# The opening of a hybrid diffusion layer: tokens loaded ahead of the scale tiles, tiles prepared ahead of the modulation's copies, shorter pauses of the side work

## The chip, the cores and the metric

One core of a Trainium2 chip runs the whole kernel. The metric is device time in microseconds, the median of three runs. The engines are TensorE (PE, its weight loads PEld), VectorE (DVE), ScalarE (ACT), GpSimd (POOL) and SyncE (SP), which here only issues DMAs. Each engine works through its own instructions in order.

## The reference

One layer over 256 latent tokens and 256 context tokens of width 2048, all in float32. Latent tokens are modulated by a vector `c`, context tokens by `c_ctx`; with one layer only the latent stream is returned. What the change touches is the start:

```python
sh1, sc1, g1, sh2, sc2, g2 = split(silu(c) @ w_ada + b_ada, 6)       # 2048 x 12288 weights
csh1, csc1, ...            = split(silu(c_ctx) @ w_ada + b_ada, 6)
h_l = (rmsnorm(x,   norm_mix) * (1 + sc1)  + sh1)  @ w_in            # 2048 x 9312
h_c = (rmsnorm(ctx, norm_mix) * (1 + csc1) + csh1) @ w_in
# latent attention and gated DeltaNet on the columns, gates, output projection,
x = x + g1 * y
x = x + g2 * conv_glu(rmsnorm(x, norm_ffn) * (1 + sc2) + sh2)        # hidden width 5504
```

## The kernel before

The width of 2048 is cut into 16 tiles of 128 rows, called tile k below. Tokens lie transposed, width on the partitions. Weights and activations are split into a high part (rounded to the matmul's format) and a low part (the rest), and a product is three matmuls: high x high, high x low, low x high.

*Opening.* `cv`, the two conditioning vectors, lands; ScalarE makes `cth` (a tanh), VectorE makes `sc` (the silu). `spread(s, q)` lays a quarter of stream s's vector out along the free axis on TensorE, and it is copied to `scb`: by VectorE for s = 0, by ScalarE for s = 1. `square` squares token quarters (`xl` latent, `xc` context), `square_sum` sums them over the width into `pss`, then come a copy `bc`, sums `msp`, a power step on GpSimd and `bc_ps`, the factors of the norm on all partitions.

*Modulation of tile pairs.* Shifts and scales of the first norm are computed here too, from 32 MB of weights. `mod_mm` multiplies four loads (`raws`, 0.5 MB each) by the vectors into `amp` and copies the row out (`row`, ScalarE); `mod_cols` sums its columns into partitions with sixteen small matmuls per half and writes `shs` or `aas` (ScalarE). This gives the shifts of a pair of tiles, and for the pairs in `SCP` (tiles 0, 1, 4, 5, 8, 9, 12, 13) also the scales (`scale_mm`). The other tiles get their scales from VectorE: `scale_dot(k, s)` is a dot product over a 1 MB tile `wt` for one stream, and `scale_fin(k)` puts bias and norm weight on the two results.

*First projection.* A loop over k. `first_hi(k)` casts the tile's weights `gr` to `gh` (ScalarE). `h_prep(k)` multiplies `xl` and `xc` by scale and norm (VectorE), makes `gl` (VectorE), the high parts of `H` with the shift (ScalarE), and the low parts (VectorE). `first_mm(k, ..., a, b)` is products a to b of the seven output tiles, each for both streams, 14 groups of three matmuls. In iteration k the kernel casts the weights of tile k+1, does two products, the products of one shift or scale group, two more products, that group's `mod_cols`, the last three products, and only then `scale_fin` and `h_prep` of tile k+1, the dots due (`dots`) and the next loads (`loads`).

*Order.* TensorE, the copies and dots of this part, and its loads go through wrappers that keep them in program order on their engine (`pe`, `oact`, `odve`, `osync`); the rest of the kernel is ordered by a planner. `load` asks for a scale tile ("w", 1 MB, four buffers), a shift group ("s", four of five 0.5 MB buffers) or a tile of the first projection's weights ("g", 0.43 MB, three buffers); all wait in SP's queue, in order, for their buffers. SP also has at most a handful of loads under way at once.

*Side work.* `ada_rest` computes the other four modulation vectors: 128 loads `rawa` of 0.5 MB, each one dot product on VectorE against one half of the scale vector, `sch`, which is loaded anew at tiles 0, 16, 48, 80 and 112. It is a generator, run in small steps beside the rest of the kernel: each `yield 1300` is a step, and callers pay for steps with `ada(ns)`. Before and after a change of the half it yields without work. 96 of the 128 dots have to be done when the output projection ends (`while ada.done < 3: ada(1)`), and `ada(WO)` after each of its 16 tiles pays for that.

The lines as the profile names them (a helper that records every operation stands as L68):

Of the kernel before, what the change touches and what calls it, by code (L numbers as in the profile page):

```python
# [25 lines left out]
N1 = 3  # L26
# [13 lines left out]
ADS = 0.3  # L40
OD = 8000
OC = 4000
WO = 2000
IK = 7000
NW = 4
SCP = (0, 2, 4, 6)
# [7 lines left out]
def hybrid_block(ctx: ExitStack, tc: tile.TileContext, io, dbg=None):  # L54
# [46 lines left out]
    dve.tensor_copy(onesr, ones.broadcast_to([P, P]))  # L101
    half = const.tile([P, 1], F32, name="half")
    dve.memset(half, -0.5)
    def vectors(pl, name, names, queue=sync):
        t = pl.tile([P, io[name].shape[1]], F32, name=name)
        queue.dma_start(t, io[name])
        pos, d = 0, {}
        for nm, n in names:
            d[nm] = t[:, pos : pos + n]
            pos += n  # L110
        return d

    off = vectors(const, "vecs", VECS, act)
    nmix, nffn, qan, kvan = off["norm_mix"], off["norm_ffn"], off["q_a_norm"], off["kv_a_norm"]
    bada = off["b_ada"]

# [136 lines left out]
    def ada_rest():  # L253


        def load(i):
            w = wr.tile([P, GR], F32, tag="raw", name="rawa", bufs=NR)
            c, n = divmod(i, 32)
            sync.dma_start(w, io["wada2"][c, (n // 16 + c) % 2, n % 16])
            return w  # L260

        parts = ad.tile([P, 2, 16], F32, name="parts")
        half, ahead = None, load(0)
        for i in range(128):
            c, n = divmod(i, 32)
            h, j = (n // 16 + c) % 2, n % 16
            if h != half:

                for _ in range(2 if i else 0):
                    yield 1300  # L270
                half, sch = h, ad.tile([P, GR], F32, tag="sch", name="sch")
                sync.dma_start(sch, Sc[h])
                for _ in range(4):
                    yield 1300
            w = ahead
            if i < 127:
                ahead = load(i + 1)
            dve.tensor_tensor_reduce(out=w, in0=w, in1=sch, scale=1.0, scalar=0.0, op0=ALU.mult, op1=ALU.add, accum_out=parts[:, h, j : j + 1])  # L278
            if n == 31:
                cs = slice(16 * c, 16 * c + 16)  # L280
                dve.tensor_tensor(out=adaT[:, cs], in0=parts[:, 0], in1=parts[:, 1], op=ALU.add)
                dve.tensor_tensor(out=adaT[:, cs], in0=adaT[:, cs], in1=bada[:, 32 + 16 * c : 48 + 16 * c], op=ALU.add)
                ada.done = c + 1
            yield 1300
# [34 lines left out]
    def spread(s, q):  # L319
        bp = psm.tile([P, 4, P], F32, tag="mm", name="scp")  # L320
        for j in range(4):
            pe.matmul(bp[:, j], sc[:, 4 * q + j, s : s + 1].broadcast_to([P, P]), ident, start=True, stop=True)
        (oact.copy if s else odve.tensor_copy)(scb[:, s, q * 512 : q * 512 + 512], bp.rearrange("p a b -> p (a b)"))
# [21 lines left out]
    def mod_cols(p, scale, amp, row):  # L345

        for j in range(2):
            col_sum(amp[:, T + 2 * j : T + 2 * j + 2], row[:, j * P : (j + 1) * P], sel[:, :2])
        for j in range(2):
            k = slice(2 * p + j, 2 * p + j + 1)  # L350
            out, mul, add = (aas, nmix[:, k], b1[:, k]) if scale else (shs, 1.0, bada[:, k])
            oact.activation(out[:, 2 * p + j], amp[:, T + 2 * j : T + 2 * j + 2], AF.Identity, bias=add, scale=mul)
# [8 lines left out]
    def scale_dot(k, s):  # L361
# [2 lines left out]
            scm[k] = pa2.tile([P, 2], F32, tag="scm", name="scm")  # L364
        junk = ad.tile([P, D], mybir.dt.bfloat16, tag="sch", name="junk")
        odve.tensor_tensor_reduce(out=junk, in0=wts[k], in1=scb[:, s], scale=1.0, scalar=0.0, op0=ALU.mult, op1=ALU.add, accum_out=scm[k][:, s : s + 1])

    def scale_fin(k):
        oact.activation(aas[:, k], scm.pop(k), AF.Identity, bias=b1[:, k : k + 1], scale=nmix[:, k : k + 1])

    def load_first(k):
        gr = pa2.tile([P, G3], F32, tag="gr", name="gr", bufs=3)
# [3 lines left out]
    def first_hi(k):  # L376

        g = [pa2.tile([P, G3], F32R, tag=n, name=n) for n in ("gh", "gl")]
        oact.copy(g[0], grs[k])
        return g  # L380

    def h_prep(k, gh, gl):

        late = k and k % 2 == 0 and k // 2 in SCP
        if late:
            odve.tensor_tensor(out=gl, in0=grs.pop(k), in1=gh, op=ALU.subtract)
        for s, xs in enumerate((xl, xc)):
            odve.scalar_tensor_tensor(out=xs[:, k], in0=xs[:, k], scalar=aas[:, k, s : s + 1], in1=(bc if k else bcp)[:, s], op0=ALU.mult, op1=ALU.mult)
        if not late:
            odve.tensor_tensor(out=gl, in0=grs.pop(k), in1=gh, op=ALU.subtract)  # L390
        for s, xs in enumerate((xl, xc)):
            oact.activation(H[s][:, k, 0], xs[:, k], AF.Identity, bias=shs[:, k, s : s + 1], scale=1.0)
        for s, xs in enumerate((xl, xc)):
            odve.scalar_tensor_tensor(out=H[s][:, k, 1], in0=xs[:, k], scalar=shs[:, k, s : s + 1], in1=H[s][:, k, 0], op0=ALU.add, op1=ALU.subtract)

    def first_mm(k, gh, gl, a, b):
        for j, (o, m) in list(enumerate(FW))[a:b]:
            hi, lo = gh[:, o : o + m], gl[:, o : o + m]
            for s in range(2):
                ps = first_ps[j][:m, s * T : s * T + T]  # L400
                pe.matmul(ps, hi, H[s][:, k, 0], start=k == 0 and s == 0, stop=False)
                pe.matmul(ps, hi, H[s][:, k, 1], start=False, stop=False)
                pe.matmul(ps, lo, H[s][:, k, 0], start=False, stop=k == KD - 1 and s == 1)
# [5 lines left out]
    def load(*what):  # L409
        for kind, n in what:  # L410
            d, f = {"w": (wts, load_scale), "s": (shifts, load_shift), "g": (grs, load_first)}[kind]
            d[n] = f(n)

    load(("w", 0))
    for q in range(4):
        ks = slice(4 * q, 4 * q + 4)
        osync.dma_start(xl[:, ks], io["xT"][:, ks])
        osync.dma_start(xc[:, ks], io["ctxT"][:, ks])
    load(("w", 1), ("s", 0), ("g", 0), ("g", 1), ("w", 2))
    pe.pinned = True  # L420


# [3 lines left out]
    def square(s, e, a, b):  # L426
        x = (xl, xc)[s][:, a:b]
        if e is oact:
            e.activation(Sq[:, a:b, s], x, AF.Square)
        else:  # L430
            e.tensor_tensor(out=Sq[:, a:b, s], in0=x, in1=x, op=ALU.mult)

    def square_sum(q):
        for j in range(4):
            pe.matmul(pss[32 * j : 32 * j + 32], ones.broadcast_to([P, 32]), Sq[:, 4 * q + j].rearrange("p a b -> p (a b)"), start=q == 0, stop=q == 3)

    def scale_mm(p):
        return mod_mm([wts[2 * p + m // 2][:, m % 2 * GR : m % 2 * GR + GR] for m in range(4)])

    for q in range(4):  # L440
        spread(0, q)
    square(0, oact, 0, 4)
    square(1, odve, 0, 4)
    for q in range(2):
        spread(1, q)
    for q in range(1, 3):
        square(0, oact, 4 * q, 4 * q + 4)
        square(1, odve, 4 * q, 4 * q + 4)
        square_sum(q - 1)
        spread(1, q + 1)  # L450
    square(0, oact, 12, 16)
    square(1, odve, 12, 14)
    square(1, oact, 14, 16)
    for q in range(2, 4):
        square_sum(q)
    bcf = bc.rearrange("p a b -> p (a b)")
    oact.copy(bcf, pss)
    msp = psa.tile([P, 4], F32, tag="aux", name="msp")
# [2 lines left out]
    ms = pa2.tile([P, 4], F32, tag="ms", name="ms", bufs=1)  # L461
    odve.tensor_scalar(out=ms, in0=msp, scalar1=1.0 / D, scalar2=EPS, op0=ALU.mult, op1=ALU.add)
    rsq(pa2, ms, ms, 4)
    later = scale_mm(0)
    bc_ps = psa.tile([P, 512], F32, tag="aux", name="bc_ps")
    for n in range(4):
        pe.matmul(bc_ps[:, n * P : n * P + P], ms[:, n : n + 1].broadcast_to([P, P]), ident, start=True, stop=True)
    bcp = bc_ps.rearrange("p (a b) -> p a b", a=2)
    mod_cols(0, True, *later)
    later = mod_mm(shifts[0])  # L470
    mod_cols(0, False, *later)
    H = [hp.tile([P, KD, 2, T], F32R, tag="h", name="h0"), ph.tile([P, KD, 2, T], F32R, tag="h", name="h1")]
    hk = first_hi(0)
    h_prep(0, *hk)
    oact.copy(bc, bcp)
    load(("s", 1), ("w", 3), ("g", 2), ("g", 3))
    first_ps = [(psm if j < 4 else psa).tile([P, 512], F32, tag="mm" if j < 4 else "aux", name="fp") for j in range(2 * N1 + 1)]

    dots = {0: (2, 2), 1: (3, 3), 3: (6,), 4: (6, 7), 5: (7,), 7: (10,), 8: (10, 11), 9: (11,), 11: (14,), 12: (14, 15), 13: (15,)}
# [3 lines left out]
    }  # L483
    for k in range(KD):

        later = None
        nxt = first_hi(k + 1) if k + 1 < KD else None
        first_mm(k, *hk, 0, 2)
        p = (k + 2) // 2
        if k == 1 or k % 2 == 0 and 0 < k < KD - 2:  # L490
            later = p, False, *mod_mm(shifts.pop(p))
        elif k % 2 and k + 1 < KD and (k + 1) // 2 in SCP:
            later = (k + 1) // 2, True, *scale_mm((k + 1) // 2)
        first_mm(k, *hk, 2, 4)
        if later:
            mod_cols(*later)
        first_mm(k, *hk, 4, 2 * N1 + 1)
        if k + 1 < KD:
            if k + 1 in scm:
                scale_fin(k + 1)  # L500
            h_prep(k + 1, *(hk := nxt))
        for c in dots.get(k, ()):
            scale_dot(c, int(c in scm))
        load(*((w[0], int(w[1:])) for w in loads.get(k, "").split()))
        if k == 13:
            tc.keep_in_program_order(act.dma_start(Sc.rearrange("h p i -> p h i"), scb[:, 0].rearrange("p (h i) -> p h i", h=2)))
# [1066 lines left out]
```

## Time and profile before

| | |
|---|---|
| median of three runs | 1846.19 us (1843.73 to 1850.49) |
| the profiled execution | 1845.3 us |
| its span | 1843.5 us |
| PE busy | 1773.1 us, 96% |
| PEld busy | 1525.7 us, 83% |
| DVE busy | 1366.4 us, 74% |
| ACT busy | 917.9 us, 50% |
| POOL busy | 45.9 us, 2% |
| loads and stores | 419.72 MB, mean 228 GB/s |
| granted clock of TensorE | 0.991 on average |

The span runs from the first to the last instruction; the execution's own time has 1.8 us around it. Busy shares are averages over stages with different limits, so the stages are read one by one.

### The profile page before, as it was taken

How to read it: one execution, taken by the hardware profiler on the slowest of the kernel's cores; microseconds unless marked ns; L12 is line 12 of the kernel's file. 1: busy time of each engine (PE TensorE's matmuls, PEld its weight loads, DVE VectorE, ACT ScalarE, POOL GpSimd, SP SyncE). 2: the span in 40 equal slices, each digit the busy share in tenths (PEclk: the TensorE clock that was granted, in tenths of full speed). 3: DMA queues.
4: the chain of work that ended last, by engine and by line, in shares of the span. 5: the costliest groups of instructions: out<-in, count | busy, mean ns of one | idle time of the engine just before them, and what ended most of it. 6: DMA issues, size and time to landing. Idle time of an engine off the chain costs nothing.

```text
span 1843.5 us, 33058 instructions
## 1 busy us (share of the span) xinstructions
PE 1773.1 (96%) x12450; PEld 1525.7 (83%) x12450; DVE 1366.4 (74%) x2758; ACT 917.9 (50%) x1876; POOL 45.9 (2%) x48
## 2 busy tenths in 40 slices
PE   7999999999998999898999989999999999999999
PEld 5787887888887888777878877888888888888887
DVE  4668899879776877575779798888877788855554
ACT  3335544445666665433346445555555555544443
POOL 0000001000000000000000000000000000000000
PEclk9999999999999999999989999999999999999999
DMA  9883688774777767887766885777766677766664
GB/s 379 349 311 110 178 241 241 215 235 132 214 229 222 217 209 227 293 287 244 250 220 206 285 297 179 254 220 223 231 197 187 212 219 221 266 194 195 201 197 120
DMA packets 195009, 419.72 MB, mean 228 GB/s; under 512 B 61280, under 2 KB 101344, under 8 KB 192416
## 3 DMA queue, kind: packets, MB, share of 16 engines
q1 hardware_dynamic: 167520, 402.19, 68.0%
q10 hardware_dynamic: 27328, 15.41, 2.8%
q8 instruction: 98, 1.61, 0.4%
q14 instruction: 63, 0.52, 0.1%
HBM read 388.57 MB, written 28.84 MB: 226 GB/s over the span
## 4 chain that ended last, share of the span: by engine, by line
PE 48%; issue 9%; DVE 2%; DMA 2%; ACT 1%; POOL 0%; SPq 0%; POOLq 0%; ACTq 0%; DVEq 0%
PE fps L68 25%; PE dps L68 13%; PE gtp L68 4%; PE brp L68 2%; PE op L68 1%; DVE wlo L121 1%; DMA raw<-in_wgate 1%; PE yp L68 1%; DMA yraw<-Ys 0%; DVE r L1264 0%; PE kp L68 0%; ACT whi L120 0%; DMA Gs<-zx 0%; POOL om L172 0%; DMA raw<-in_wgd 0%
## 5 line engine op out<-in xcount | busy, mean ns | idle before, releaser
L121 DVE TENSOR_TENSOR wlo<-raw,whi 128x512 fp32r<-128x512 f32 (+1 forms) x940 | 634.5, 686 | 209.7 <-ACT whi L120 202.0
L120 ACT CAST whi<-raw 128x512 fp32r<-128x512 f32 (+1 forms) x940 | 572.9, 618 | 420.8 <-PE dps L68 112.4
L68 PE MATMUL fps<-H,whi 128*128 128x512 f32 x1376 | 481.5, 398 | 1.7 <-DVE H L1416 1.7
L68 PE MATMUL fps<-H,wlo 128*128 128x256 f32 x1376 | 374.3, 282 | 0.6 <-DVE wlo L121 0.6
L68 PEld LDWEIGHTS fps<-H,whi 128*128 128x128 f32 x1376 | 253.8, 189 | 57.9 <-issue 2.0
L68 PEld LDWEIGHTS fps<-H,wlo 128*128 128x128 f32 x1376 | 259.3, 188 | 8.7 <-DVE wlo L121 1.1
L68 PE MATMUL gtp<-h,whi 128*128 128x512 f32 x640 | 234.7, 402 | 5.1 <-ACT whi L120 5.1
L68 PE MATMUL mmp<-h,whi 128*128 128x512 f32 x640 | 228.9, 400 | 0.0
L68 PE MATMUL dps<-GB,whi 128*128 128x512 f32 x560 | 195.9, 391 | 0.0
L278 DVE CUSTOM_DVE_ANT_0 rawa<-rawa,sch 128x1024 f32<-128x1024 f32 x128 | 156.2, 1222 | 44.0 <-DMA rawa<-in_wada 43.1
L68 PE MATMUL gtp<-h,wlo 128*128 128x256 f32 x640 | 175.7, 285 | 5.5 <-DVE wlo L121 5.2
L68 PE MATMUL mmp<-h,wlo 128*128 128x256 f32 x640 | 176.6, 282 | 0.0
L68 PE MATMUL dps<-GB,wlo 128*128 128x256 f32 x560 | 155.3, 282 | 0.0
L68 PEld LDWEIGHTS gtp<-h,whi 128*128 128x128 f32 x640 | 120.8, 190 | 31.5 <-ACT whi L120 6.3
L68 PEld LDWEIGHTS mmp<-h,whi 128*128 128x128 f32 x640 | 119.1, 188 | 26.2 <-issue 0.4
L68 PEld LDWEIGHTS gtp<-h,wlo 128*128 128x128 f32 x640 | 121.3, 190 | 13.2 <-DVE wlo L121 8.7
L68 PEld LDWEIGHTS dps<-GB,whi 128*128 128x128 f32 x560 | 105.2, 188 | 21.7
L68 PEld LDWEIGHTS mmp<-h,wlo 128*128 128x128 f32 x640 | 120.5, 188 | 2.8 <-issue 0.6
L68 PEld LDWEIGHTS dps<-GB,wlo 128*128 128x128 f32 x560 | 105.9, 189 | 0.6
L68 PE MATMUL fp<-h,gh 128*128 128x256 f32 (+1 forms) x448 | 86.6, 291 | 7.9 <-DVE h L68 5.9
L68 PEld LDWEIGHTS fp<-h,gh 128*128 128x128 f32 (+1 forms) x448 | 69.2, 187 | 15.1 <-DVE h L68 8.0
L513 ACT COPY fx<-fps 128x256 f32<-128x256 f32 x86 | 31.9, 374 | 68.3 <-PE fps L68 68.2
(561 smaller groups left out, 2561.9 us busy)
## 6 DMA issues: line engine op xcount, KB each, us to landing
rawa<-in_wada SPq DMA_DIRECT2D x128, 512.0 KB, 4.7
raw<-in_wgate SPq DMA_DIRECT2D x82, 512.0 KB, 4.3
raw<-in_wval SPq DMA_DIRECT2D x82, 512.0 KB, 4.8
raw<-in_wdown SPq DMA_DIRECT2D x80, 512.0 KB, 4.3
wt<-in_wadas SPq DMA_DIRECT2D x16, 1024.0 KB, 9.9
raw<-in_wadab SPq DMA_DIRECT2D x32, 512.0 KB, 8.5
raw<-in_wgm SPq DMA_DIRECT2D x32, 512.0 KB, 4.9
raw<-in_wgd SPq DMA_DIRECT2D x32, 512.0 KB, 6.1
```

What stands on the lines that cost most here:

```text
L68: i = f(*a, **k)
L120: act.copy(hi, raw)
L121: dve.tensor_tensor(out=lo, in0=raw, in1=hi, op=ALU.subtract)
L278: dve.tensor_tensor_reduce(out=w, in0=w, in1=sch, scale=1.0, scalar=0.0, op0=ALU.mult, op1=ALU.add, accum_out=parts[:, h, j : j + 1])
L513: act.copy(out, ps[:M, T:])
```

## The change

The vectors' load goes to SP's queue. The tokens are loaded before the first scale tile; the fourth scale tile and the third tile of first-projection weights are asked for ahead of the second shift group. The spreads of the second stream are interleaved with the square sums, and the last of them takes the place of the scale products beside the power step; these follow `bc_ps`. In the loop `h_prep` of tile k+1 comes ahead of tile k's products and modulation, but for tile 2 and for the tiles 4, 8 and 12, where it stays behind. In iterations 3, 7 and 11 the scale products come first of all; in iterations 1 and 2 the shift products come behind four products, elsewhere behind two as before. `scale_fin` becomes one VectorE instruction right behind a tile's second dot. The side work yields once, not twice, before a change of the half, and three times, not four, after it; `WO` is 1500 instead of 2000.

```diff
-WO = 2000
+WO = 1500
@@ vectors
-    def vectors(pl, name, names, queue=sync):
+    def vectors(pl, name, names):
-        queue.dma_start(t, io[name])
+        sync.dma_start(t, io[name])
-    off = vectors(const, "vecs", VECS, act)
+    off = vectors(const, "vecs", VECS)
@@ ada_rest
-                for _ in range(2 if i else 0):
+                for _ in range(1 if i else 0):
                     yield 1300
                 half, sch = h, ad.tile([P, GR], F32, tag="sch", name="sch")
                 sync.dma_start(sch, Sc[h])
-                for _ in range(4):
+                for _ in range(3):
                     yield 1300
@@ scale_dot
+        if s:
+            odve.tensor_scalar(out=aas[:, k], in0=scm.pop(k), scalar1=nmix[:, k : k + 1], scalar2=b1[:, k : k + 1], op0=ALU.mult, op1=ALU.add)
-    def scale_fin(k):
-        oact.activation(aas[:, k], scm.pop(k), AF.Identity, bias=b1[:, k : k + 1], scale=nmix[:, k : k + 1])
@@ loads of the opening
-    load(("w", 0))
     for q in range(4):
         ...
-    load(("w", 1), ("s", 0), ("g", 0), ("g", 1), ("w", 2))
+    load(("w", 0), ("w", 1), ("s", 0), ("g", 0), ("g", 1), ("w", 2), ("w", 3), ("g", 2))
@@ spreads and squares
     for q in range(4):
         spread(0, q)
-    square(0, oact, 0, 4)
-    square(1, odve, 0, 4)
-    for q in range(2):
-        spread(1, q)
-    for q in range(1, 3):
-        square(0, oact, 4 * q, 4 * q + 4)
-        square(1, odve, 4 * q, 4 * q + 4)
-        square_sum(q - 1)
-        spread(1, q + 1)
-    square(0, oact, 12, 16)
-    square(1, odve, 12, 14)
-    square(1, oact, 14, 16)
-    for q in range(2, 4):
-        square_sum(q)
+        if q % 2:
+            square(0, oact, 2 * q - 2, 2 * q + 2)
+            square(1, odve, 2 * q - 2, 2 * q + 2)
+    for q in range(4):
+        square_sum(q)
+        if q < 3:
+            spread(1, q)
+        if q < 2:
+            square(0, oact, 4 * q + 8, 4 * q + 12)
+            square(1, odve, 4 * q + 8, 4 * q + 12 - 2 * q)
+        if q == 1:
+            square(1, oact, 14, 16)
@@ behind the power step
-    later = scale_mm(0)
+    spread(1, 3)
     ...
-    mod_cols(0, True, *later)
+    mod_cols(0, True, *scale_mm(0))
     ...
-    load(("s", 1), ("w", 3), ("g", 2), ("g", 3))
+    load(("s", 1), ("g", 3))
@@ the loop over k
+        p, late = k // 2 + 1, k % 2 and k + 1 < KD and (k + 1) // 2 in SCP
+        if k + 1 < KD:
+            nxt = first_hi(k + 1)
+            if not late and k != 1:
+                h_prep(k + 1, *nxt)
+        at = 0 if late else 4 if k < 3 else 2
+        first_mm(k, *hk, 0, at)
         later = None
-        nxt = first_hi(k + 1) if k + 1 < KD else None
-        first_mm(k, *hk, 0, 2)
-        p = (k + 2) // 2
         if k == 1 or k % 2 == 0 and 0 < k < KD - 2:
             later = p, False, *mod_mm(shifts.pop(p))
-        elif k % 2 and k + 1 < KD and (k + 1) // 2 in SCP:
-            later = (k + 1) // 2, True, *scale_mm((k + 1) // 2)
-        first_mm(k, *hk, 2, 4)
+        elif late:
+            later = p, True, *scale_mm(p)
+        first_mm(k, *hk, at, at + 2)
         if later:
             mod_cols(*later)
-        first_mm(k, *hk, 4, 2 * N1 + 1)
+        first_mm(k, *hk, at + 2, 2 * N1 + 1)
         if k + 1 < KD:
-            if k + 1 in scm:
-                scale_fin(k + 1)
-            h_prep(k + 1, *(hk := nxt))
+            if late or k == 1:
+                h_prep(k + 1, *nxt)
+            hk = nxt
```

## Rows read from the trace of the kernel before

**Rows 1.** Stretches: length, busy of PE, PEld, DVE, ACT, POOL; clock, DMA share, GB/s.
```profile
0.00:33.58 33.58, 20.17 (x234) 13.70 (x234) 11.10 (x25) 12.87 (x23) 2.19 (x8) 0.99 0.96 367
33.58:149.40 115.82, 109.17 (x1152) 93.45 (x1153) 79.34 (x114) 41.17 (x90) 0.00 (x0) 0.99 0.83 323
957.00:1112.00 155.00, 142.70 (x812) 122.06 (x813) 133.12 (x281) 78.79 (x171) 0.78 (x2) 0.96 0.74 246
```

**Rows 2.** The opening: start, length, engine, line, operation, tiles, idle before.
```profile
0.73 0.42 ACTq L106 DMA_DIRECT2D vecs<-in_vecs  x1
...
8.04 0.23 ACT L305 ACTIVATE cth<-cv 128x32 f32<-128x32 f32 x1 [4.61 <-DMA cv<-in_cv]
...
8.86 7.42 PE L68 MATMUL scp<-ident,sc 128*128 128x128 f32 x48 [8.86 <-DVE sc L308]
...
19.58 1.16 PE L68 MATMUL scp<-ident,sc 128*128 128x128 f32 x8
...
22.36 1.57 PE L68 MATMUL pss<-sq,ones 128*32 128x512 f32 x8 [0.64 <-ACT sq L68]
...
26.75 1.16 PE L68 MATMUL bc_ps<-ident,ms 128*128 128x128 f32 x8
...
32.50 0.36 PE L68 MATMUL fp<-h,gh 128*96 128x256 f32 x1 [1.74 <-ACT h L68]
```

**Rows 3.** TensorE across the ends of tiles 2 and 5.
```profile
56.72 0.28 PE L68 MATMUL fp<-h,gh 128*96 128x256 f32 x1
...
57.66 0.36 PE L68 MATMUL fp<-h,gh 128*96 128x256 f32 x1 [0.66 <-DVE h L68]
...
77.16 0.40 PE L68 MATMUL fp<-h,gh 128*128 128x256 f32 x2
...
77.39 0.28 PE L68 MATMUL fp<-h,gl 128*128 128x256 f32 x1
...
77.72 0.36 PE L68 MATMUL fp<-h,gh 128*96 128x256 f32 x1
...
78.94 0.36 PE L68 MATMUL fp<-h,gh 128*96 128x256 f32 x1 [0.86 <-DVE h L68]
```

**Rows 4.** VectorE and ScalarE at the end of tile 5.
```profile
74.42 2.29 DVE L68 CUSTOM_DVE_ANT_0 junk<-wt,scb 128x2048 bf16<-128x2048 f32 x1
...
77.16 0.51 ACT L68 ACTIVATE h<-xl,shs 128x256 fp32r<-128x256 f32 x1 [2.35 <-DVE xl L68]
```

**Rows 5.** TensorE at the shift groups of tiles 2, 4 and 12.
```profile
49.70 1.74 PE L68 MATMUL amp<-raw,csf 128*32 128x256 f32 x24
...
52.07 0.64 PE L68 MATMUL amp<-raw,csf 128*32 128x256 f32 x8 [0.63 <-DMA raw<-in_wadab]
...
52.64 0.50 PE L68 MATMUL fp<-h,gh 128*128 128x256 f32 x2
...
66.59 1.93 PE L68 MATMUL amp<-raw,csf 128*32 128x256 f32 x32
...
68.46 0.39 PE L68 MATMUL fp<-h,gh 128*128 128x256 f32 x1
...
127.98 0.64 PE L68 MATMUL amp<-raw,csf 128*32 128x256 f32 x8 [0.55 <-DMA raw<-in_wadab]
```

**Rows 6.** Stretches of the loads, columns as in Rows 1.
```profile
6.50:52.10 45.60, 37.36 (x404) 28.16 (x405) 24.02 (x39) 16.84 (x32) 1.02 (x1) 0.96 1.01 403
26.30:36.30 10.00, 6.99 (x98) 5.18 (x91) 5.10 (x10) 5.55 (x13) 0.10 (x1) 0.84 0.99 386
36.30:52.10 15.80, 14.47 (x160) 11.74 (x160) 10.87 (x13) 3.80 (x8) 0.00 (x0) 0.99 1.01 415
78.94:108.60 29.66, 28.10 (x313) 23.77 (x313) 19.50 (x29) 10.27 (x23) 0.00 (x0) 1.00 0.88 344
```

**Rows 7.** Costliest groups: the side work's dots; landing of `sch`.
```profile
L278 DVE CUSTOM_DVE_ANT_0 rawa<-rawa,sch 128x1024 f32<-128x1024 f32 x128 | 156.2, 1222 | 44.0 <-DMA rawa<-in_wada 43.1
...
DMA to landing us min/median/max: 3.2/5.6/7.7
```

## The prediction

> **What bounds the kernel now.** I read the stretches first, then the order of work inside the first one. TensorE is busy for 96% of the span, so time can only come from the stretches where it is not. Two matter. In the first 33.58 us it is busy for 20.17, and from there to 149.40, the sixteen tiles of the first projection, it loses 115.82 - 109.17 = 6.65 us [rows 1]. The output projection and the change to the feed-forward part lose 12.3 us more (155.00 - 142.70), but the diff touches that stretch only through the pace of the side work.
>
> The opening is a chain: `cv` lands, `cth` runs at 8.04, the first spread starts at 8.86, the square sums end at 22.36 + 1.57 = 23.93, `bc_ps` follows at 26.75, and the first product starts at 32.50 [rows 2]. Inside the tiles the reader is to see two kinds of stall. At a tile's end the first product with `H` high parts goes out and the second waits for the low part that VectorE makes: products leave every 0.12 us (77.16 to 77.39 is two of them), yet from 56.72 to 57.66 is 0.94, which is 0.82 lost, and 77.39, 77.72, 78.94 hold 0.21 + 1.10 = 1.31 lost [rows 3]. The second kind is a shift group whose last load is late: 49.70 to 52.64 for what takes 66.59 to 68.46, or 1.87, elsewhere; and once more at 127.98, after 0.55 of idling [rows 5]. That late load is no accident of its own place: up to 52.1 the DMA engines are full (share 1.01, 403 GB/s), so in this part the loads set the time, and TensorE only after it [rows 6].
>
> **The opening.** Three moves. The vectors' load goes from ScalarE's queue to the head of SP's, the tokens' eight loads stand ahead of the first scale tile, and the last spread and the scale products change places around the power step. Now `cv` is first in its queue with no megabyte beside it. How early it lands, the trace does not show: at worst at the old 8.0, at best 3.9, if it is asked for at 0.73 like the vectors before it [rows 2] and takes the 3.2 us of the quickest half of the scales [rows 7]. I take 4.1, close to the best, since only the small vectors stand beside it, and so a first spread, 0.82 after it as before, at about 5.0 instead of 8.86. From spread to the end of the sums took 15.07; the eighth spread leaves that stretch (1.16, of which about 1.1 is its step) and so does the 0.64 wait for a square [rows 2], which leaves 13.3 and an end at 18.3. The tokens land 1 MB earlier, some 2.5 us at 415 GB/s, and so keep up. From there to the first product took 32.50 - 23.93 = 8.57. The scale products (1.93, the length of such a group at 66.59 [rows 5]) now stand behind `bc_ps` instead of under the power step, and their row copy and column sum are bare: plus 2.5. First product at 18.3 + 11.1 = 29.4, 3.1 earlier. With `cv` at its worst it is 0.8 later than before, at best 3.3 earlier.
>
> Little of this reaches the end, because the loads come next. Tile 2's shift group ran its first product at 49.70 and got its last quarter at 52.07 [rows 5]. The diff gives the queue nothing less to fetch by then. What it can recover is the weak stretch: 26.3 to 36.3 moved 386 GB/s where the next 15.8 us moved 415 [rows 6], because SP was waiting there for buffers of the first shift; with the fourth scale tile and a first-projection tile asked for ahead of that wait, 10 x (1 - 386/415) = 0.70 us comes back. Bounds: nothing, or 1.3 if the first 20 us do better too. So the last quarter lands near 51.3. TensorE arrives at 49.70 - 3.1 + 1.42 = 48.0 (it now does four products first, two more, 12 x 0.118 = 1.42), and would want that quarter 1.4 later, at 49.4. It still waits, and the opening has a cushion of 1.9 us: a first spread up to 6.9, or a worse stall at tile 2 (only one product, not three, is left there to cover the copies: up to 1.42), costs nothing. Beyond that each us costs one, so `cv` at its worst (3.9 later than I take it) costs 2.0.
>
> **The products before the wait.** Those two products are then done before the load and not after it: 1.42 gained in tile 2. In tile 1 the same move is hidden in the cushion.
>
> **The tiles.** Preparing tile k+1 now stands ahead of tile k's products and of the modulation's copies, except for tile 2 and for the tiles 4, 8, 12 whose scale comes from TensorE. The cause of a tile's stall is visible at 77.16: ScalarE waited 2.35 for `xl`, which stood behind two products with the scale rows of 2.29 each on VectorE [rows 4]. In the new order that work is queued a tile earlier. It still waits for the high part's cast, which needs a buffer from the tile before, so it starts at a tile's start and takes 0.9 + 1.0 + 0.9, about 3 us of at least 5. The stalls at tiles 3, 7, 11 (0.82 each) and 6, 10, 14 (1.31 each) go: 2.46 + 3.93 = 6.39. For tiles 4, 8 and 12 the scale products move to the head of the tile, which leaves five products (3.5 us) instead of three behind the column sums; these did not stall. The `scale_fin` copies move from ScalarE to VectorE, six of some 0.2 us, under products. The wait at 127.98 goes too: SP's queue gets its first-projection buffers back a tile earlier, 0.55.
>
> Can the loads follow? A period of four tiles took 29.66 us at 344 GB/s [rows 6]; without its stalls (1.31 + 0.82) it takes 27.5 and asks for 371, under the 415 that the queue has shown.
>
> **The pauses.** Two of six pauses are dropped at each of the four switches of the scale half, and one of four at the start: nine steps of 1300, so side work comes earlier by some three loads by 450 us and five by 740. `WO` = 1500 takes 16 x 500 = 8000, about six steps, back out of the output projection, so that the 96 loads needed are done at the same place. I count 0 for this, covered by idle VectorE; without cover five dots of 1.22 and their share of the 43.1 us that 128 dots waited for loads (0.34) are 7.8 [rows 7].
>
> **Sum.** 0.70 + 1.42 + 6.39 + 0.55 = 9.06. The profiled execution took 1845.3 (span 1843.5), 0.9 under the median of the runs shown. 1845.3 - 9.1 = 1836.2, and I say 1836.0. 0.5% of the median is 9.2 us and is about what a measurement can tell from no change, so the forecast lies at that bound.
>
> **Rivals.**
> (a) The copies stand behind the prepared tile. ScalarE now does cast and `H` of tile k+1 ahead of the row copy that the column sums need. If `xl` is still behind a 2.29 us dot then, TensorE waits at the column sums. My count leaves about 1 us of room in tiles 4, 6, 8, 10 and 12. Missed by 1 us in all five: 5 back, 1841. Against it: the dots were done by the tile's end before as well.
> (b) The loads come slower than 415 when more of them are asked for together. At the 367 GB/s of the first 33.58 us [rows 1] the 45.6 us at 403 need 4.5 more, so tile 2 loses 4.5 and keeps 1.42 + 0.82; a period needs 344 x 29.66 / 367 = 27.8 instead of 27.5, which leaves about 4.7 of the later stalls' gain, and 0.55: 2.9 less, 1842. For it speaks the weak stretch of 386; against it 415 over 15.8 us [rows 6]. The Trainium skill (HBM Reference, Specifications) states about 358 GB/s as a core's share when both cores of a pair stream, and more for a core alone; by that figure the loads would bind every period and I estimate 1845. The trace, at 415, agrees with the core alone.
> (c) The rest gains too. Two loads fewer in the output projection, where TensorE idles 12.3 us; a third of that back is 4: 1832.
> (d) The earlier side work costs where VectorE is on the path: half of 7.8 to all of it, 1840 to 1844.
> (e) Slower than before: the switches. With a pause less, the dots reach the new half before it lands, 5.6 us after its issue at the median [rows 7]. VectorE works in order, so its splits stand behind that dot and TensorE behind the splits. Four switches bare are 22.4, and 1858.6. It decides from 9.1 / 4 = 2.3 us at each. Against it: in all five only 0.6 was waited so far.
>
> **Numbers.** Forecast 0.48, with a range of its own of 1832.5 to 1839.5; (a) 0.17; (b) 0.03; (c) 0.14; (d) 0.13; (e) 0.05. Below 1837.0 lie seven tenths of the forecast, (c), and slips of (a) and (d): 0.51 faster. Above 1855.4 lies little but (e) and what I have not thought of: 0.05. Same: 0.44. The range 1830 to 1843 leaves out (b), (e) and the ends of (c) and (d).
>
> **What would show it.** Right: the first spread near 5, the first product near 29.4, a wait for a shift load still in tile 2 and ending near 51.3, products 0.12 apart across the ends of tiles 3, 6, 7, 10, 11 and 14, the tiles done near 140 instead of 149.4, and later stretches of equal length. Wrong: a first spread after 7, a wait of TensorE for the row copy in even tiles (a), a load share at 1.0 through the later tiles (b), or the stretch from 450 to 740 longer by more than 3 us (d).

## The result, and the profile after

The changed kernel takes 1838.56 us (median of 12 executions, 1832.18 to 1844.14) where the kernel before takes 1846.7 (12, 1841.2 to 1851.92): a ratio of 0.9950, 95% interval 0.9937 to 0.9963. The medians lie 8.1 us apart (0.44%); by the ratio it is 0.50%, right at the bound that the prediction names. The prediction said 1836.0 with 1830 to 1843. The profiled execution took 1835.39, span 1833.5, granted clock 0.992, and lies 3.2 under the median; its places are read here, its end is not.

First the stretches, as in [rows 1, 6], of the kernel after (length; busy of PE, PEld, DVE, ACT, POOL; clock, DMA share, GB/s):

```profile
0.00:31.34 31.34, 21.84 (x234) 14.79 (x234) 11.13 (x25) 13.08 (x23) 2.19 (x8) 0.99 0.96 369
31.34:140.50 109.16, 106.81 (x1152) 93.32 (x1153) 81.44 (x122) 38.89 (x82) 0.00 (x0) 0.99 0.91 356
...
3.00:8.00 5.00, 3.75 (x17) 3.78 (x18) 1.75 (x9) 1.28 (x2) 0.00 (x0) 1.00 0.96 299
26.30:36.30 10.00, 6.35 (x60) 5.50 (x57) 6.47 (x9) 4.58 (x10) 0.00 (x0) 0.83 1.02 411
36.30:52.70 16.40, 14.09 (x150) 10.84 (x149) 12.02 (x18) 4.21 (x9) 0.00 (x0) 1.00 1.02 415
...
75.82:103.30 27.48, 27.48 (x316) 23.85 (x315) 20.18 (x31) 9.95 (x22) 0.00 (x0) 1.00 0.98 391
```

The tiles lose 109.16 - 106.81 = 2.35 us instead of 6.65, and end at 140.50 instead of 149.5. The last line runs from the start of tile 6 to 0.19 behind that of tile 10 (103.11), so the period of four tiles takes 27.29 us, where it took 29.66 before [rows 6]; TensorE is busy in all of it. One row more of the kernel before is needed beside the third line, its own stretch from 3 to 8 us:

```profile
3.00:8.00 5.00, 0.00 (x0) 0.00 (x0) 0.48 (x4) 0.43 (x1) 0.00 (x0) 1.00 1.00 388
```

The loads start slower after the change, 299 GB/s against 388, and make only a part of it good later, 411 against 386 [rows 6].

The opening, which answers to [rows 2]: ScalarE's `cth`, then TensorE (start, length, engine, line, operation, tiles, idle before):

```profile
3.44 0.23 ACT L305 ACTIVATE cth<-cv 128x32 f32<-128x32 f32 x1 [0.49 <-DMA cv<-in_cv]
```

```profile
4.25 6.71 PE L68 MATMUL scp<-ident,sc 128*128 128x128 f32 x32 [4.25 <-DVE sc L308]
...
17.14 1.19 PE L68 MATMUL pss<-sq,ones 128*32 128x512 f32 x8
...
20.85 1.16 PE L68 MATMUL bc_ps<-ident,ms 128*128 128x128 f32 x8 [0.31 <-POOL ms L172]
21.93 1.93 PE L68 MATMUL amp<-wt,csf 128*32 128x256 f32 x32
...
27.02 0.64 PE L68 MATMUL amp<-raw,csf 128*32 128x256 f32 x8 [0.64 <-DMA raw<-in_wadab]
...
30.25 0.36 PE L68 MATMUL fp<-h,gh 128*96 128x256 f32 x1 [1.75 <-ACT h L68]
```

The spread starts 4.6 us earlier and the sums end 5.6 earlier, at 18.33, but the first product comes only 2.25 earlier: the first shift group, which had its loads in time before, now waits for its last quarter at 27.02.

Then tile 2, which answers to [rows 3, 5], and the end of tile 5, where 1.31 had been lost:

```profile
49.00 0.64 PE L68 MATMUL amp<-raw,csf 128*32 128x256 f32 x8 [0.33 <-DMA raw<-in_wadab]
50.19 0.64 PE L68 MATMUL amp<-raw,csf 128*32 128x256 f32 x8 [0.55 <-DMA raw<-in_wadab]
51.47 0.64 PE L68 MATMUL amp<-raw,csf 128*32 128x256 f32 x8 [0.64 <-DMA raw<-in_wadab]
52.74 0.64 PE L68 MATMUL amp<-raw,csf 128*32 128x256 f32 x8 [0.63 <-DMA raw<-in_wadab]
53.31 0.50 PE L68 MATMUL fp<-h,gh 128*128 128x256 f32 x2
...
56.07 1.93 PE L68 MATMUL amp<-wt,csf 128*32 128x256 f32 x32
...
75.71 0.28 PE L68 MATMUL fp<-h,gl 128*128 128x256 f32 x1
75.82 0.40 PE L68 MATMUL fp<-h,gh 128*96 128x256 f32 x2
```

Each of the four quarters of tile 2's shifts is waited for, 2.15 us together, and the first product behind the group goes out at 53.31, where it was 52.64. Tile 3 starts at 56.07. At 75.82 tile 6 begins 0.11 after the product ahead of it; tiles 3, 7, 10, 11 and 14 begin in the same way, and no idle time over 0.1 us is left between 53.4 and 140.5. (Tile 3's first work is its scale products, at 56.07.)

From the tiles' end to the last instruction the two profiled executions take the same: 1694.0 before, 1693.0 after. In the experiments it ranges from 1686.8 to 1701.2, and the second half of them is about it.

### The profile page after: what moved, and what is told of

Its sections match the earlier page's. It is cut to its first block, busy times and chain, and to the rows that moved or that the text cites. A ratio compares the mean times of both kernels' runs of the same rounds, so it can differ in the third digit from the quotient of the medians.

```text
span 1833.5 us, 33054 instructions
## 1 busy us (share of the span) xinstructions
PE 1773.5 (97%) x12450; PEld 1526.8 (83%) x12450; DVE 1367.2 (75%) x2766; ACT 914.6 (50%) x1868; POOL 45.5 (2%) x48
## 4 chain that ended last, share of the span: by engine, by line
PE 49%; issue 9%; DVE 2%; DMA 2%; ACT 1%; POOL 0%; SPq 0%; POOLq 0%; ACTq 0%; DVEq 0%
PE fps L68 26%; PE dps L68 13%; PE gtp L68 4%; PE brp L68 2%; PE op L68 1%; DVE wlo L121 1%; PE yp L68 1%; DMA Gs<-zx 1%; DMA raw<-in_wgate 1%; DVE r L1264 0%; PE kp L68 0%; ACT whi L120 0%; DMA jit<-Xo 0%; POOL om L172 0%; DMA raw<-in_wgd 0%
## 5 line engine op out<-in xcount | busy, mean ns | idle before, releaser
L68 PEld LDWEIGHTS dps<-GB,whi 128*128 128x128 f32 x560 | 105.1, 188 | 21.7
```

Of the source, the lines that this page charges most:

```text
L68: i = f(*a, **k)
```

## The experiments

My theories at the start: the loop's new order gives the whole gain at the tiles, and the load stream takes back what the opening wins; the rival is that the opening shares in it. Of the pauses I thought that they had shortened the attention stretch, which is 5 us shorter in the profile after.

| kernel | time (us) | ratio to before, 95% | first product | tile 2's last shift load | tiles end | from there to the end | projection and transition |
|---|---|---|---|---|---|---|---|
| before | 1846.7 | | 32.50 | 52.03 | 149.5 | 1694.0 | 103.8 |
| after | 1838.56 | 0.9950 (0.9937-0.9963) | 30.25 | 52.70 | 140.5 | 1693.0 | 105.1 |
| 1 loop only | 1839.28 | 0.9958 (0.9944-0.9973) | 32.29 | 52.05 | 140.3 | 1691.0 | 101.3 |
| 2 opening only | 1845.31 | 0.9991 (0.9979-1.0003) | 29.93 | 53.75 | 152.6 | 1694.3 | 100.5 |
| 3 pauses and `WO` only | 1849.25 | 1.0013 (1.0002-1.0024) | 33.0 | 52.27 | 149.9 | 1701.2 | 104.3 |
| 4 after, old pauses and `WO` | 1834.38 | 0.9939 (0.9926-0.9952) | 29.99 | 52.38 | 140.2 | 1690.8 | 100.7 |
| 5 after, a load less | 1836.86 | 0.9954 (0.9941-0.9967) | 29.2 | 49.31 | 138.3 | 1694.8 | 103.4 |
| 6 after, shifts behind two | 1838.71 | 0.9975 (0.9959-0.9991) | 29.9 | 52.65 | 144.2 | 1692.6 | 105.0 |
| 7 after, old pauses, new `WO` | 1840.99 | 0.9973 (0.9961-0.9985) | 29.7 | 52.08 | 139.9 | 1698.9 | 105.5 |
| 8 as 4, shifts of tile 2 behind six | 1836.65 | 0.9954 (0.9936-0.9971) | 30.5 | 52.83 | 139.6 | 1687.4 | 100.1 |
| 9 after, new pauses, old `WO` | 1832.81 | 0.9923 (0.9899-0.9947) | 30.18 | 52.46 | 140.2 | 1691.0 | 99.7 |
| 10 as 9, shifts of tile 2 behind six | 1831.06 | 0.9915 (0.9888-0.9942) | 30.35 | 52.58 | 139.3 | 1690.5 | 98.3 |
| 11 as 4, vectors on ScalarE's queue | 1838.21 | 0.9949 (0.9929-0.9969) | 32.35 | 51.75 | 140.6 | 1686.8 | 100.5 |
| 12 as 4, again | 1836.16 | 0.9942 (0.9925-0.9959) | 30.16 | 52.41 | 140.2 | 1688.8 | 100.8 |

The times are medians of 5 to 12 executions. The ratios are to runs of the kernel before that were made beside them, with medians of 1846.8 us (kernels 1 to 4), 1845.85 (5 to 8) and 1847.27 (9 to 12); so between these groups the ratios compare, rather than the times. The places are read in the one profiled execution of each. The last column runs from the output projection's first product to the feed-forward part's first; the one before it includes it.

### 1. The loop alone

The kernel before with the new loop and with the scales finished on VectorE; opening and pauses as they were.

```diff
 (before)
+    the loop over k, and scale_dot with tensor_scalar, as in the change
```

> The kernel before with the new loop alone (tiles prepared ahead, two more products ahead of the shifts in tiles 1 and 2, scale groups first, the scale's last step on VectorE); opening and pauses as before. My theory: the loads up to tile 2's shift group set the time there, so the first product stays at 32.5, the last quarter of that group lands near 52.0 as before, TensorE finds it there with next to no wait, and the tiles end near 141 instead of 149.5: some 8.5 of the 9.0 us that the whole change brings there. The rival theory, that the earlier opening is worth its 2.3 us at the first product: the tiles end near 143 at best.

Its last product of the tiles, which starts at 149.19 in the kernel before and at 140.19 in the kernel after:

```profile
139.97 0.28 PE L68 MATMUL fp<-h,gl 128*128 128x256 f32 x1
```

The tiles end at 140.3. The loop alone gives all of the 9 us, with a first product 2 us later than in the whole change.

### 2. The opening alone

```diff
 (before)
+    vectors' load on SP, order of the opening's loads, spreads and squares as in the change
```

> The kernel before with the new opening alone (vectors' load on the other queue, tokens first, spreads and squares in the new order, scale and weight tile ahead of the second shift group); loop and pauses as before. My theory: the first product comes near 30.3 instead of 32.5, and all of it is lost again at tile 2, whose shift group lands at 52.0 to 52.7: the tiles end between 149 and 150.2, no gain, same time within 1 us. The rival theory: they end 2 us earlier, near 147.3.

The first product comes 2.6 us earlier and the tiles end 3.1 later than before, more than I expected. Two things do it. The last quarter of tile 2's shifts landed at 53.75, 1.7 later than in the kernel before (1.05 later than in the whole change, whose loads of the opening are the same; the second load of the tokens, ahead of everything in which the two kernels differ, landed at 8.93 here and at 7.70 there, so that this much differs from one execution to another). And behind these waits TensorE worked at half its clock, as its rows and then its stretches (length, PE busy, clock, DMA share, GB/s) show:

```profile
50.05 0.64 PE L68 MATMUL amp<-raw,csf 128*32 128x256 f32 x8 [1.32 <-DMA raw<-in_wadab]
...
53.79 0.86 PE L68 MATMUL amp<-raw,csf 128*32 128x256 f32 x8 [0.64 <-DMA raw<-in_wadab]
54.58 0.80 PE L68 MATMUL fp<-h,gh 128*128 128x256 f32 x2
```

```profile
53.00:55.00 2.00, 1.36 (x14) 0.77 1.03 391
55.00:57.00 2.00, 2.00 (x11) 0.50 0.65 265
```

Two products end 0.80 after they start instead of 0.50, and the 12 from 54.58 on take 2.93 us where the 12 at 53.31 of the kernel after take 1.69: 1.24 more. The clock is at its lower level, 1.2 GHz, after gaps of 1.32, 0.55, 0.62 and 0.64 with 0.64 of work after each of the first three.

### 3 and 4. The pauses alone, and all but the pauses

```diff
 (3: before; 4: after, the other way round)
-WO = 2000
+WO = 1500
-                for _ in range(2 if i else 0):
+                for _ in range(1 if i else 0):
-                for _ in range(4):
+                for _ in range(3):
```

> The kernel before with the pauses and the pace of the side work alone. My theory: the tiles end at 149.5 as before; the stretch from the attention to the scan, where VectorE waited 5.1 for one side-work load and TensorE then 2.7, becomes some 5 us shorter, and the scan and output projection give 3 to 4 back: 0 to 2 faster in all. The rival theory, that those stretches moved because everything before them moved: no stretch behind the tiles changes by more than 1 us.

> The changed kernel with the old pauses and the old pace. My theory: the tiles end near 140.5 as in the changed kernel, the attention stretch keeps the old stall (5 longer), scan and output projection keep their old length: 0 to 2 slower than the changed kernel in all, so about 0.995 to 0.996 of the kernel before. The rival theory: the stretches behind the tiles are those of the changed kernel.

My theory on the pauses fell. The attention stretch (from 452.1 to 740.5 before, 288.4; from 443.2 to 726.5 after, 283.3) takes 289.5 in kernel 3, and kernel 3 is slower than before by 0.13%. Without the pauses' edit the changed kernel is not slower but, if anything, quicker: 1834.38, ratio 0.9939 against 0.9950, with intervals that overlap. The output projection, with the transition to the feed-forward part, takes 105.1 and 104.3 us with the edit, 100.7 without it.

### 5. A load less in the opening

The changed kernel without the load of scale tile 3, for which tile 2's data stand in: the scales of tile 3 are other numbers.

```diff
     def load_scale(k):
+        if k == 3:
+            return wts[2]
```

> The changed kernel without the load of scale tile 3 (tile 2's data stand in for it, so the scales of tile 3 are other numbers). My theory: the arrival of the opening's load stream sets tile 2's wait. Then the last quarter of tile 2's shifts, which landed at 52.70, lands some 2.4 us earlier, near 50.3, the four waits of together 2.15 us in tile 2 nearly go, and the sixteen tiles end near 138.4 instead of 140.5. Rival, that TensorE's own work or VectorE sets it: the tiles end within 0.3 of 140.5.

```profile
48.62 1.93 PE L68 MATMUL amp<-raw,csf 128*32 128x256 f32 x32
...
52.74 0.31 PE L68 MATMUL amp<-sel,row 128*32 128x2 f32 x16 [0.57 <-ACT row L68]
```

As the theory said: landing at 49.31, no wait for a load left in tile 2, tiles done at 138.3. In that place the loads set the time; what TensorE waits for now is the row copy, 0.57. The whole kernel's time does not show the 2.2 us (ratio 0.9954 against 0.9950, intervals of 0.0013 to either side).

### 6. The shifts behind two groups of products

```diff
-        at = 0 if late else 4 if k < 3 else 2
+        at = 0 if late else 2
```

> The changed kernel with the shift groups of tiles 1 and 2 behind two groups of products instead of four. My theory: the last quarter lands near 52.7 in either, the group ends near 53.4, and two groups of products more (12 products, 1.68 us at the full clock) stand behind it: the tiles end near 142.2. If the longer waits also bring TensorE's granted clock down, as in the kernel with the opening alone, where it was 0.50 at 55 to 57 us, up to 1.4 more: 143.6. Rival, that the place of the group is worth nothing: 140.5.

The first quarter of the group, and two stretches (length, PE busy, clock, DMA share, GB/s):

```profile
48.99 0.64 PE L68 MATMUL amp<-raw,csf 128*32 128x256 f32 x8 [2.29 <-DMA raw<-in_wadab]
```

```profile
53.00:55.00 2.00, 2.00 (x14) 0.50 1.05 422
55.00:57.00 2.00, 2.00 (x25) 0.50 0.99 407
```

The tiles end at 144.2, 3.7 later than after the change: the dearer branch, and 0.6 more. The quarter landed at 52.65, as before the edit, so the place of the group and the clock make the difference. TensorE waited 2.29, 0.55, 0.63 and 0.17, and the granted clock was 0.50 from 53 to 57. The place of the shift group is worth more than the 1.42 that I gave it, because with it the clock stayed up: in the kernel after, with waits of 0.33, 0.55, 0.64 and 0.63, it is 1.00 throughout 36.3 to 52.7. In the whole time the ratio is 0.9975 against 0.9950, with intervals that just overlap.

### 7 and 9. The two edits of the pauses, one at a time

```diff
 (7: after, with the old pauses)
-                for _ in range(1 if i else 0):
+                for _ in range(2 if i else 0):
-                for _ in range(3):
+                for _ in range(4):
 (9: after, with the old WO)
-WO = 1500
+WO = 2000
```

> The changed kernel with the old pauses (two and four) and the new WO of 1500: one of the two edits that the kernel with neither lacked. If WO sets the output projection's cost, that projection takes near 97 us (97.26 with both edits, 90.40 with neither) and the time is near 1838; if the pauses set it, 90 to 91 us and a time near 1834.

> The changed kernel with its new pauses and the old WO of 2000: the other of the two edits. So far: neither edit 1834.4, WO of 1500 alone 1841.0, both 1838.6. My theory: WO of 1500 costs some 6 us where the pauses are old, at and behind the output projection (projection and transition together 100.7 us with neither, 105.5 with WO alone, 105.1 with both), and the new pauses give up to 2.4 back ahead of it. Then projection and transition take near 101 us and the time is 1832 to 1834.5. Rival, that the two edits only hurt when together or that the new pauses themselves cost: projection and transition near 105 and 1838.

`WO` is what costs. With the old pauses 1500 takes 1840.99 against 1834.38 and 1836.16 (kernels 4 and 12) for 2000; with the new pauses 1838.56 against 1832.81. As ratios that is 0.9973 against 0.9939 and 0.9942, with intervals apart, and 0.9950 against 0.9923, with intervals that overlap at their ends. From the output projection's first product to the last instruction, the part that `WO` can touch, the five profiles with 1500 take 836.7 to 838.4 us, the eight changed or partly changed kernels with 2000 832.1 to 834.4, and the kernel before 836.1. All five profiles with 1500 have a projection and transition of 103.4 to 105.5 us, the eight with 2000 one of 98.3 to 101.3. The kernel before, with 2000 too, has 103.8; there TensorE waits 1.6 us for `wlo`, the low parts of the projection's weights, and in kernel 1 it does not, but what brings that wait was not tried. In kernel 7 it was not the projection that grew, as I had expected, but the transition behind it (92.4 and 13.0): the rest of the 96 dots is then done there.

The place is seen in VectorE's dots from 980 to 1120 us; the first group is the kernel after, the second kernel 9 (count; min, median, max ns; idle time before them):

```profile
L278 DVE CUSTOM_DVE_ANT_0 rawa<-rawa,sch x17: 1217/1225/1227, 1000.0 to 1086.0; 128x1024 f32<-128x1024 f32 x17
...
  DMA rawa<-in_wada: 17.6, 11
```

```profile
L278 DVE CUSTOM_DVE_ANT_0 rawa<-rawa,sch x23: 1211/1217/1226, 1002.4 to 1086.4; 128x1024 f32<-128x1024 f32 x23
...
  DMA rawa<-in_wada: 3.7, 4
```

and in one stretch of each, the kernel after first, then kernel 9, and in TensorE's dearest wait of the kernel after:

```profile
1045.00:1065.00 20.00, 18.50 (x102) 15.17 (x101) 16.37 (x30) 7.86 (x17) 0.00 (x0) 1.00 0.81 269
```

```profile
1045.00:1065.00 20.00, 20.00 (x115) 17.28 (x114) 19.12 (x41) 9.29 (x20) 0.00 (x0) 1.00 0.90 329
```

```profile
1086.16 0.39 PE L68 MATMUL ops<-MA,wlo 128*128 128x256 f32 x1 [1.99 <-DVE wlo L121]
```

With 17 dots instead of 23 VectorE stands longer, not shorter, for their loads: 17.6 us instead of 3.7 (kernel 4, with 19 dots, 6.4). It works in order, so `wlo` stands behind the waiting dot, and TensorE waits for it: 5.1 us in seven waits in the kernel after, none in kernels 4 and 9, and the projection itself takes 97.3 us against 90.4 and 90.6. The DMA engines are not the reason, for they move less, 269 GB/s against 329, and a load takes no longer from its issue to its landing (median 5.0 us against 5.6): it is issued too late for its dot. Why fewer dots leave their loads later was not tried.

The pauses themselves seem to give a little: kernel 9 against 4 and 12 is 1.6 to 3.4 us, and the kernel after against kernel 7, the same pair with 1500, is 2.4 us (ratios 0.9950 and 0.9973), with intervals that overlap in both. That is not settled, and the attention stretch does not tell either: two executions of one kernel (4 and 12) have 285.7 and 283.7 there.

### 8 and 10. The shifts of tile 2 behind six groups

```diff
-        at = 0 if late else 4 if k < 3 else 2
+        at = 0 if late else 6 if k == 2 else 4 if k < 3 else 2
```

> The changed kernel with the old pauses and WO, and tile 2's shift group behind six groups of products instead of four. My theory: the group still ends near 53.2 with its last quarter's landing, one group of products and the column sums are left behind it instead of three, less a wait of up to 0.5 for the row's copy: tile 3 begins 1.2 to 1.7 us earlier, the tiles end near 138.8 and the time is near 1833. Rival: tile 3's shift or scale group then waits for its own loads and the gain is gone by tile 4: tiles end near 140.2, time 1834.4.

> The kernel with the new pauses and the old WO, and tile 2's shift group behind six groups of products. Tiles end near 139.5, up to 1 us ahead of the kernel with four; the time 0 to 1 us under that kernel's, 1831 to 1834. Rival, that what is won at the tiles is lost in the side work: the same time or above.

The tiles end at 139.6 and 139.3, 0.6 and 0.9 earlier than with four. Of the wait 0.57 and 0.27 are left, and 0.54 comes anew: the scale products at the head of tile 3 wait for ScalarE's copy of the shifts. For kernel 8 I had expected 138.8 and 1833; its time is 1836.65, a ratio of 0.9954 where kernel 4 has 0.9939, with intervals that overlap. Kernel 10 has the lowest time of all, 1831.06 (ratio 0.9915), but its interval and kernel 9's are nearly the same. That the tiles end up to 0.9 us earlier is what the profiles say and the times cannot.

### 11 and 12. The vectors back on ScalarE's queue, and kernel 4 again

```diff
 (11: kernel 4 with)
-    off = vectors(const, "vecs", VECS)
+    off = vectors(const, "vecs", VECS, act)
```

> The changed kernel with the old pauses and WO, and the vectors' load issued on ScalarE's queue again, as before the change, ahead of the condition vector's. If the issue on SP ahead of the tokens' loads (0.44 us) and the small rows there made the load stream late, the second tokens' load lands near 7.4 (7.9), the last quarter of tile 2's shifts near 52.0 (52.4) and the tiles end 0.4 earlier, 139.8. Rival, that the tokens' smaller rows themselves make the start slow: landings as before within 0.2, the condition vector 0.4 later, tiles end 140.2. The time within 1 us of 1834.4 in either.

> The changed kernel with the old pauses and WO once more, beside the three others on one chip: 1834.4 in the first look. Expected 1833 to 1836, and in the profile a tile end of 140 to 140.5 and a landing of tile 2's last shift quarter within 0.5 of 52.4, which shows how far two executions of one kernel differ there.

Kernel 11's stretch and its opening:

```profile
3.00:8.00 5.00, 0.07 (x1) 0.10 (x1) 0.96 (x8) 1.30 (x3) 0.00 (x0) 1.00 0.98 352
```

```profile
7.93 6.29 PE L68 MATMUL scp<-ident,sc 128*128 128x128 f32 x32 [7.93 <-DVE sc L308]
...
27.83 1.93 PE L68 MATMUL amp<-raw,csf 128*32 128x256 f32 x32
...
32.35 0.36 PE L68 MATMUL fp<-h,gh 128*96 128x256 f32 x1 [1.74 <-ACT h L68]
```

The start of the stream explains some 0.7 us: with the vectors' load off SP's queue it runs at 352 GB/s instead of 299, which over 5 us is 0.64 us' worth of loads at 415, and tile 2's last quarter lands at 51.75 instead of 52.41 (kernel 12, same chip). These are single executions, but all nine profiles with the vectors on SP's queue and the full loads have it later, from 52.08 to 53.75. But `cv`, now behind the vectors and beside the tokens, lands at 7.10 instead of 3.32, and the first product is back at 32.35. Tile 2's wait for loads is gone, and the tiles end at 140.6 all the same. I had expected 0.4 earlier. TensorE starts the shift group at 50.97 here, at 49.66 and 48.71 in kernels 4 and 12, so what the loads were given is lost at TensorE's arrival. The time, 1838.21, is above the 1834.4 and 1 us that I had expected; kernel 12 beside it has 1836.16, with intervals that overlap. The second execution of kernel 4's program agrees with the first at the tiles (52.41 and 52.38; 140.2 twice).

## Why the prediction was right, and where not

**The size at the tiles: right by two errors.** I summed 9.06; the tiles end 9.0 earlier. But two of its terms were off, by 1.3 to 1.4 us each, in opposite directions: the loads gave -0.67 instead of 0.70, the stalls 8.2 instead of 6.39 + 0.55. That the sum still fits is luck.

**0.70 from the weak stretch: failed.** The stretch behaved as predicted, 411 GB/s instead of 386. The step that failed is that nothing else in the stream changes. The start, 3 to 8 us, fell from 388 to 299, and the quarter predicted for 51.3 landed at 52.70, 0.67 later than before. Kernel 11 puts 0.66 of these 1.4 us on the vectors on SP's queue, ahead of the tokens; the rest stays open (with the tokens first its stream still starts at 352, not 388). I had counted their move as what lets `cv` land early (3.41 for a predicted 4.1), and not as what it puts ahead of the tokens.

**The first product at 29.4.** Spread at 5.0 and sums at 18.3: measured 4.25 and 18.33. The first product came 0.85 late, at 30.25; 0.64 of that is the wait for the first shifts' last quarter, for which I had no term. As said, none of it reaches the end: kernel 1 without the new opening ends its tiles at 140.3. So the cushion was real, and the opening's part of the change is worth nothing at the tiles. The prediction also counts six `scale_fin` copies of some 0.2 us; there are eight, of 0.39 us on ScalarE before and 0.29 on VectorE after, a slip that the sum does not feel.

**1.42 for two products ahead of the wait: right.** From the end of the shift group to tile 3, 53.31 to 56.07 is 2.76; before it was 52.64 to 57.54 (the start at 56.72 and the 0.82 lost behind it), or 4.90. The difference of 2.14 is 1.42 plus 0.72 of tile 3's stall. What I did not see is that the old place under the new opening would also have cost clock: kernel 6 lost 3.7.

**6.39 and 0.55 for the stalls: right, and undersized.** All six stalls and the wait at 127.98 are gone. The period of four tiles fell by 29.66 - 27.29 = 2.37, for a predicted 1.31 + 0.82 = 2.13. From tile 3's start to the end of the tiles the gain is 91.9 - 84.4 = 7.5, where the sum had 6.1 left. Of the difference 0.95 lies behind the first product of tile 10: 107.38 to 149.48 became 103.11 to 140.48, 4.73 for a predicted 1.10 + 0.82 + 0.55 + 1.31 = 3.78. Two terms are seen there: the shift group of tile 12 lost 0.75 before (125.92 to 128.54 is 2.62, elsewhere 1.87), where the sum took only its 0.55 of idling, and tile 15 took 5.50 before and 5.14 after, for which the sum had nothing. Loads followed, at 391 GB/s in the period for a predicted 371. So rival (b) fell, and (a) too: in the kernel after TensorE waits for no row copy in an even tile (where tile 2's loads are not late it does, 0.36 in kernel 1 and 0.57 in kernel 5). The Trainium skill (Perfetto Trace Analysis, Roofline) puts a single core's ceiling at about 435 GB/s, and the 415 of the full stretch lies under it.

**0 for the pauses: failed.** The kernels without the edit gain 12.4 and 11.1 us on the kernel before (kernels 4 and 12, in medians), 2 to 3 more than the tiles, and the kernel after gains 8.1. What is lost between them is `WO` (5.7 us between the kernel after and kernel 9), less what the shorter pauses may give back (1.6 to 3.4). "Later stretches of equal length" did not hold either: from the projection's first product to the end kernels 4 and 12 take 833.2 and 833.6, the kernel before 836.1 and the kernel after 838.3. So the forecast of 1836.0 came near by a second pair of opposite slips, both behind the tiles. I took the six steps out of the output projection as neutral, because the 96 dots would be done at the same place, and in rival (c) even as a gain. They are done there (98 of the dots at the projection's end, 97 before), but with a waiting VectorE, whose dots the trace shows, and not covered by an idle one. Rival (d) had a cost of the right size at the wrong place: it looked for it in side work that comes earlier, and it came with side work that was spread thinner. Of the predicted earlier loads, three by 450 us did not show (17 in both kernels) and five by 740 did (59 for 54). The switches of rival (e) did not bite: with the new pauses VectorE waits for `sch` once in each of the six profiles, 0.5 to 2.0 us between 636 and 652 (1.35 in the kernel after), where the kernels with the old pauses have no such wait; their own lie in the projection, at most 2.7 in kernel 7.

**The chances.** The prediction gave 0.51 to a gain of 0.5% and more and 0.44 to less. The ratio of 0.9950 lies on that bound, so the measurement does not tell which of the two came. With `WO` left at 2000 (kernel 9) the gain is 0.77% (0.53 to 1.01).

## What to carry to other kernels

Where loads and an engine meet, here at tile 2, find out first which of them comes last: with the late first product of kernel 11 earlier loads gained nothing, with the early one of the kernel after a load less gained 2.2 us (kernel 5), and an earlier TensorE alone only waited longer. What a load is moved in front of is part of the move's price, also for small loads: some 0.7 us of 182 KB ahead of the tokens came out at the end of the stream, 50 us later (one execution each). And a pace parameter of side work is not neutral because the sum of the work is the same: read what stands behind it on its in-order engine, and change it in a run of its own.

## What was not expected of the hardware

- TensorE's clock fell to 0.50 (1.2 GHz) while the engine was not idle but worked 0.64 in every 1.2 to 1.3 us (kernels 2 and 6, after a first gap of 1.32 or 2.29); with a first gap of 0.33 and the same rhythm behind it (the kernel after) it stayed at 1.00. The products behind it cost 1.24 us more in kernel 2.
- The small condition vector landed 2.7 us after its issue when nothing large was under way (kernel after, issued at 0.73, landed at 3.41), and 5.9 us after it when it was issued 0.45 later, behind the vectors on its own queue and beside the tokens' first loads (kernel 11). Which of the two delays it was not tried.
- One program's median hides executions from 1829 to 1843 us (kernel 11, ten of them), while the tiles of nearly the same program end at the same tenth of a microsecond in two profiles (kernels 4 and 12). The 2.0 us between those two executions lie behind the tiles; whether it is so for the others no profile shows.
